# Layer 1 of a hybrid decoder trunk: weight copies ordered ahead of a rounding, and a last output block in two groups with three stores per row tile

## The chip, the cores and the metric

The kernel runs on one core of a Trainium2 chip. A core has five engines, each with an instruction stream of its own that it works off in order: TensorE (PE, matrix products into banks of the accumulator memory), VectorE (DVE), ScalarE (ACT), GpSimd (POOL) and SyncE (SP, which here issues transfers only). Transfers (DMA) are issued to a queue by one of the engines. The metric is the time of one execution on the device in microseconds; the median of several runs is given.

## The reference

Two layers are applied to `x` (256 rows, 1024 columns), and then a last RMS norm. Each layer normalises its input, multiplies it with one 1024 x 3584 matrix, and feeds three kinds of heads: eight attention heads A with a dilated mask, an RG-LRU recurrence B of 256 channels, and four stick-breaking attention heads C. Their gated outputs are joined, multiplied with a 1024 x 1024 matrix and added to the input.

```python
def hybrid_layer(x, cos, sin, norm_gain, w_in, ...):
    hn = rms_norm(x, norm_gain)
    proj = jnp.einsum('bsd,de->bse', hn, w_in)
    a_q, a_k, a_v, a_g, b_x, b_g, c_q, c_k, c_v, c_g = jnp.split(proj, _in_split_points(), axis=-1)
...
    y_a = dilated_attention(qa, ka, va)... * jax.nn.silu(a_g)
    y_b = rg_lru_branch(b_x, ...) * jax.nn.silu(b_g)
    y_c = stick_breaking_attention(qc, kc, vc)... * jax.nn.silu(c_g)
    y = jnp.concatenate([y_a, y_b, y_c], axis=-1)
    return x + jnp.einsum('bse,ed->bsd', y, w_out)

def reference(x, ..., final_gain):
...
    for l in range(DEPTH):
        h = hybrid_layer(h, ...)
    return rms_norm(h, final_gain)

def rms_norm(x, gain):
    xf = x.astype(jnp.float32)
    xf = xf * lax.rsqrt(jnp.mean(xf * xf, axis=-1, keepdims=True) + EPS)
    return (xf * gain.astype(jnp.float32)).astype(x.dtype)
```

## The kernel before

**Tiling.** The 256 rows are two tiles of 128 (`t`), the 1024 columns eight blocks of 128 (`k`). Every operand of a large product is split into a rounded half (`hi`) and the remainder (`lo`), and `mm3` adds three products: hi x hi, hi x lo, lo x hi. In the projections of layer 1 (`l == 0` in the code; layer 2 is `l == 1`) the result of 256 columns for all rows sits in one bank, two blocks of 128 columns beside each other.

**Weights.** They come as 18 chunks a layer, 1 MB each. `load_chunk` takes a chunk in two loads of 512 KB on SP's queue, into a ring of five staging buffers `st` (pool `wst`). ACT rounds each in two pieces of 512 columns (`whi`, line 109), and DVE subtracts to get the rest (`wlo`, line 110). A staging buffer is free for the next load when both of its pieces are subtracted; SP's queue is in order. Chunks are asked for two ahead of their use (`ask`, `AHEAD`).

**Order.** PE's instructions run in the order of the code. Those of the other engines are put in order by a scheduler with a model of the durations; `dep(a, b)` adds an edge, so that `a` is put behind `b`. `table` loads one of ACT's two function tables.

**The place in layer 1.** After the first query and key chunks of A, `split_qk` rounds q and k, `conv` projects the input of the LRU (`bxp`) and convolves it on DVE, and meanwhile PE transposes the stick-breaking weights `sw` (`turned`, lines 458 to 463). Each of three `turned` groups fills a bank `s` (pool `at`, four banks), which ACT copies to `wv` (line 463). Then `second` runs the dilated scores (`dil_scores`, line 514), which take four `s` banks. `it`, `th`, `rt` belong to the LRU, whose gates (line 573) also take `s` banks.

**The end of layer 2.** The output product has 1024 rows of weights, taken in two halves (`out_mm`; first the outputs of B and C with half of A, then the rest), and 512 columns at a time (`n2`). The first halves of all four blocks `(t, n2)` come ahead of the second ones, so four banks stay open: one of pool `at`, three of pool `pp`; pool `yp` has one bank `y`, used by the value products (line 426) and read by line 412. When a block is done, DVE adds it to the residual `xres` (line 689) and `finish` makes the last norm: ACT squares and sums, DVE multiplies with the gain, ACT takes the logarithm and the exponential for the root (`lnv`, `rstd`, line 83), then DVE scales the first 512 columns and ACT the last 512, and SP and ACT store them (line 244). For the very last block the residual is added in two pieces of 320 and 192 columns (`LATE`); DVE squares and sums the first piece (line 231), ACT the second (line 232).

Of the kernel before, what the change touches and what calls it, by code (L numbers as in the profile page):

```python
# [15 lines left out]
P = 128  # L16
S = 256
D = 1024
# [10 lines left out]
AHEAD = 2  # L29
WST = 5  # L30
SCR = 7
LATE = 320
WARM = 7

C_DG = 0
# [13 lines left out]
def trunk_kernel(ctx: ExitStack, tc: tile.TileContext, x, first_x, first, wpack, prm_d, gatew, gains, consts, rope, out):  # L49
# [32 lines left out]
    def tab(*a, **k):  # L82
        i = dep(act.activation(*a, **k), loaded["load"])  # L83
        loaded["users"].append(i)
        return i
# [10 lines left out]

    xx, xh, xl = x_tile()

    split = {}

    def load_chunk(l, c):
        hi = wsp.tile([P, 2048], F32R, name="whi", tag="whi")
        lo = wsp.tile([P, 2048], F32R, name="wlo", tag="wlo")
        for i in range(2):
            st = wst.tile([P, 1024], F32, name="st", tag="st")
            nc.sync.dma_start(out=st, in_=wpack[l, c][:, i * 1024:(i + 1) * 1024])
            for j in range(0, 1024, 512):
                ws, ss = slice(i * 1024 + j, i * 1024 + j + 512), slice(j, j + 512)
                split[l, c] = act.activation(hi[:, ws], st[:, ss], AF.Copy)  # L109
                dve.tensor_sub(lo[:, ws], st[:, ss], hi[:, ws].bitcast(F32))  # L110
        return hi, lo

# [91 lines left out]
        act.activation(hi, ps, AF.Copy)  # L204
        dve.tensor_sub(lo, ps, hi.bitcast(F32))

    def mm3(ps, lhs, rhs, ks, first, last):
        lh, ll = lhs
        rh, rl = rhs
        seq = [(a, b, k) for a, b in ((lh, rh), (lh, rl), (ll, rh)) for k in ks]  # L210
        for i, (a, b, k) in enumerate(seq):
            pe.matmul(ps, a(k), b(k), start=first and i == 0, stop=last and i == len(seq) - 1)  # L212

    last = {}

    def finish(t, n2):
        ot = last["ot", t, n2] = scr(512)
        x_t = xres[:, t, n2 * 512:n2 * 512 + 512]
        if n2 == 0:
            sq = wk.tile([P, 3], F32, name="sq3", tag="sq3", bufs=2)  # L220
            last["sq", t] = sq, wk.tile([P, 1], F32, name="ss", tag="ss", bufs=2)
        sq, ss = last["sq", t]
        if n2 == 0:
            act.activation(scr(512), x_t, AF.Square, accum_out=sq[:, 0:1])
            gps.tensor_scalar(ss, sq[:, 0:1], 1.0 / D, EPS, ALU.mult, ALU.add)
            dve.tensor_mul(ot, x_t, last["gf"][:, 0:512])
            return
        c, late = 0, ss
        if t == 1:
            c, late = LATE, sq[:, 2:3]  # L230
            dve.tensor_tensor_reduce(scr(c), x_t[:, 0:c], x_t[:, 0:c], 1.0 / D, ss, ALU.mult, ALU.add, late)
        act.activation(scr(512 - c), x_t[:, c:512], AF.Square, scale=D ** -0.5, accum_out=sq[:, 1:2])
        dve.tensor_mul(ot, x_t, last["gf"][:, 512:1024])
        ln = wk.tile([P, 1], F32, name="lnv", tag="lnv", bufs=2)
        tab(ln, sq[:, 1:2], AF.Ln, bias=late)
        rstd = wk.tile([P, 1], F32, name="rstd", tag="rstd", bufs=4)
        tab(rstd, ln, AF.Exp, scale=-0.5)
        for half, queue in ((0, nc.sync), (1, act)):
            o = last["ot", t, half]
            if half == 0:  # L240
                dve.tensor_scalar(o, o, rstd, None, ALU.mult)
            else:
                act.activation(o, o, AF.Copy, scale=rstd)  # L243
            queue.dma_start(out=out[t * P:(t + 1) * P, half * 512:half * 512 + 512], in_=o)

    def normed(t):
        rstd = rms_stats(t, gps)
# [50 lines left out]
    for l in range(L):  # L298
# [14 lines left out]
        def proj_b(c, mid=None, to=None, sc=1.0):  # L313
            pair = c in PAIRED[l]
            hi, lo = [a.rearrange("p (k c) -> p k c", c=256) for a in weights(l, c, AHEAD - 1 if mid else AHEAD)]
            if pair:
                flat = None if to is not None else scr(512)
                to = [v2(flat)[:, b, :] for b in range(2)] if to is None else to
            else:
                flat = bank(pp, "pp")  # L320
            for b in range(2):
                cs = slice(b * P, b * P + P)
                if pair:
                    ps = bank(pp, "pp")
                    seq = [(0, k) for k in range(NK - 1)] + [(1, k) for k in range(NK)] + [(0, NK - 1)]
                    for i, (is_lo, k) in enumerate(seq):
                        if is_lo:
                            pe.matmul(ps[:, 0:S], lo[:, k, cs], xh[:, k, :], start=False, stop=False,  # L328
                                      skip_group_check=True)
                        else:  # L330
                            pe.matmul(ps, hi[:, k, cs], xx[:, k].rearrange("p h t -> p (h t)"), start=i == 0,  # L331
                                      stop=i == len(seq) - 1, skip_group_check=True)
                    low = wk.tile([P, S], F32, name="low", tag="low", bufs=2)
                    act.activation(low, ps[:, S:2 * S], AF.Copy, scale=sc)  # L334
                    if sc == 1.0:
                        dve.tensor_add(to[b], ps[:, 0:S], low)
                    else:
                        dve.scalar_tensor_tensor(to[b], ps[:, 0:S], sc, low, ALU.mult, ALU.add)
                else:
                    mm3(flat[:, b * 256:(b + 1) * 256], [lambda k, a=a: a[:, k, cs] for a in (hi, lo)],  # L340
                        [lambda k, a=a: a[:, k, :] for a in (xh, xl)], range(NK), True, True)
                if b == 0 and mid:
                    mid()
                    ask(l, c)
            return flat
# [111 lines left out]
        def turned(tiles, h0, gs, to):  # L457
            for g in gs:
                tp = bank(at, "s")
                for i in range(4):  # L460
                    h, j = divmod(4 * g + i, 3)
                    pe.transpose(tp[:, i * P:(i + 1) * P], tiles[h0 + h][:, j * P:(j + 1) * P], ident)  # L462
                act.activation(to[g], tp, AF.Copy)

        def turned_tile():
            wv = wk.tile([P, 1536], F32, name="wv", tag="wv", bufs=1)
# [148 lines left out]
        split_qk(0, ("yl0", "yh0"))  # L615
        sw_t, sw_heads = turned_tile()
        conv(lambda: turned(sw, 0, (0,), sw_t))
        turned(sw, 0, (1, 2), sw_t)
        y_c = {}

        def second():
# [28 lines left out]
        table(SIGM)  # L650
        silu(ag[:, 0:2, :], ps)
        emit_y(y_c["y"], ag[:, 0:2, :], 4, 2)
        silu(ag[:, 2:4, :], proj_b(CH_AG + 1))
        table(LN_EXP)

        def out_mm(ps, w, t, half, ks, first, last):
            v = [a.rearrange("p (k c) -> p k c", c=512) for a in w]
            ts_ = slice(t * P, t * P + P)
            mm3(ps, [lambda k, a=a: a[:, k, ts_] for a in ys[half]],
                [lambda k, a=a: a[:, k, :] for a in v], ks, first, last)  # L660

        o_ps = {}
        for n2 in range(2):
            w = weights(l, CH_O + n2)
            for t in range(NT):
                o_ps[t, n2] = bank(at, "s") if (t, n2) == (0, 0) else bank(pp, "pp")
                out_mm(o_ps[t, n2], w, t, 0, range(4), True, False)
                if (t, n2) == (0, 0):
                    y_c["p"] = dil_transposes(4)
                if (t, n2) == (0, 1):  # L670
                    emit_y(values(va, y_c["p"], 4), ag[:, 2:4, :], 6, 2)
# [4 lines left out]
        for t in range(NT):  # L676
            if t == 1 and l == 0:
                next_x = x_tile()
                xn0 = normed(0)
            for n2 in range(2):  # L680
                cs = slice(n2 * 512, n2 * 512 + 512)
                for ks in ((0, 1), (2, 3)):
                    out_mm(o_ps[t, n2], ow[n2], t, 1, ks, False, ks[0] == 2)
                    if (l, t, n2, ks[0]) == (0, 1, 1, 0):
                        turn(xn0, 0, *next_x[1:])
                parts = ((0, LATE), (LATE, 512)) if l > 0 and (t, n2) == (1, 1) else ((0, 512),)
                for c0, c1 in parts:
                    c = slice(n2 * 512 + c0, n2 * 512 + c1)
                    dve.tensor_add(xres[:, t, c], o_ps[t, n2][:, c0:c1], xres[:, t, c])  # L689
                if l > 0:  # L690
                    finish(t, n2)

# [106 lines left out]
```

## Time and profile before

| | us |
|---|---|
| median of three runs | 248.68 (248.48 to 250.25) |
| the profiled execution, whole | 248.61 |
| its span, first to last instruction | 246.5 |
| PE busy / DVE busy / ACT busy in the span | 238.6 / 193.3 / 170.5 |
| POOL busy | 11.3 |
| mean granted clock of PE, as a share of full speed | 0.995 |

The profile is one execution. A row of the chain or of the timeline begins with the start and the length in microseconds, both counted from the span's beginning; then come the engine, the operation with its line in the kernel, the output and input by their names in the program, the shapes and the count of equal instructions. A bracket at the end gives how long the engine had idled before and what released it. PEld is PE's weight load, and SPq, ACTq and POOLq are the engines' issuing of transfers. The chain follows the work that ended last back to the start, and so shows what set the time; the groups sum over the whole span and show only what is much.

### The profile page before, as it was taken

The numbers are of one execution on the slowest core, as the hardware profiler recorded it, in microseconds if no ns is written. First come the engines' busy times: TensorE is split into PE (matmuls) and PEld (weight loads), VectorE is DVE, ScalarE is ACT, GpSimd is POOL, SyncE is SP. The second block draws the span as 40 slices with busy tenths as digits, with TensorE's granted clock in tenths as the row PEclk, the third lists the DMA queues.
The fourth block names the chain that finished last, engine by engine and source line by source line (L and its number), as shares of the span: only waits on it lengthen the run. The fifth ranks groups of instructions, "written<-read, shape, count | busy, mean of one in ns | idle before, by whom it ended". The sixth has DMA issues, their size and how long they took to land.

```text
span 246.5 us, 4741 instructions
## 1 busy us (share of the span) xinstructions
PE 238.6 (97%) x1753; PEld 212.4 (86%) x1753; DVE 193.3 (78%) x454; ACT 170.5 (69%) x368; POOL 11.3 (5%) x45
## 2 busy tenths in 40 slices
PE   7999999999999999999999999999999999999990
PEld 4889999999998899878889988888889889987870
DVE  3875599999999789986693666999999967985253
ACT  3867989854688499974672775876589749992142
POOL 0027100000100000000000000000010000000000
PEclk9999999999999999999999999999999999999997
DMA  6999799377737632277258387506462752000022
GB/s 208 390 289 412 313 316 322 112 237 255 229 102 233 231 96 78 89 237 251 108 166 256 101 297 256 201 6 204 148 205 56 233 228 85 3 0 0 3 85 85
DMA packets 13174, 43.90 MB, mean 178 GB/s; under 512 B 1632, under 2 KB 2144, under 8 KB 13152
## 3 DMA queue, kind: packets, MB, share of 16 engines
q1 hardware_dynamic: 12384, 42.30, 50.9%
q10 hardware_dynamic: 576, 0.79, 0.9%
q0 software_dynamic: 192, 0.52, 0.8%
q8 instruction: 14, 0.23, 0.3%
q14 instruction: 8, 0.07, 0.1%
HBM read 42.03 MB, written 1.05 MB: 175 GB/s over the span
## 4 chain that ended last, share of the span: by engine, by line
PE 94%; DMA 2%; DVE 1%; ACT 1%; SPq 0%; issue 0%; ACTq 0%
PE pp L212 51%; PE pp L331 11%; PE s L212 9%; PE pp L328 5%; PE s L169 4%; PE s L462 3%; PE s L514 2%; PE y L426 2%; DMA st<-first 2%; PE pp L169 2%; PE s L442 1%; PE pp L426 1%; PE s L573 1%; PE s L260 1%; DVE xres L689 0%; ACT scr L243 0%
## 5 line engine op out<-in xcount | busy, mean ns | idle before, releaser
L110 DVE TENSOR_TENSOR wlo<-st,whi 128x512 fp32r<-128x512 f32 x132 | 84.0, 684 | 12.6 <-ACT whi L109 12.3
L109 ACT ACTIVATE whi<-st 128x512 fp32r<-128x512 f32 x132 | 73.8, 628 | 20.2 <-DMA st<-w_pack 7.5
L212 PE MATMUL pp<-xx,whi 128*128 128x256 f32 x480 | 63.8, 285 | 0.0
L212 PEld LDWEIGHTS pp<-xx,whi 128*128 128x128 f32 x480 | 59.7, 191 | 1.3 <-ACT whi L109 0.4
L212 PE MATMUL pp<-xx,wlo 128*128 128x256 f32 x240 | 33.7, 283 | 0.0
L212 PEld LDWEIGHTS pp<-xx,wlo 128*128 128x128 f32 x240 | 31.0, 192 | 0.0
L331 PE MATMUL pp<-xx,whi 128*128 128x512 f32 x112 | 29.2, 396 | 0.0
L331 PEld LDWEIGHTS pp<-xx,whi 128*128 128x128 f32 x112 | 20.1, 189 | 3.9 <-ACT scr L83 0.3
L83 ACT ACTIVATE pr<-scr,mn 128x128 f32<-128x128 f32 (+1 forms) x32 | 14.1, 442 | 8.4 <-DVE mn L521 8.4
L77 ACT ACT_TABLE_LOAD x13 | 16.7, 1283 | 1.9 <-PEq L792 1.7
L328 PEld LDWEIGHTS pp<-xx,wlo 128*128 128x128 f32 x112 | 15.3, 190 | 1.1
L328 PE MATMUL pp<-xx,wlo 128*128 128x256 f32 x112 | 15.6, 282 | 0.0
L212 PE MATMUL pp<-whi,yh 128*128 128x512 f32 x48 | 14.4, 400 | 0.0
L212 PE MATMUL pp<-wlo,yh 128*128 128x512 f32 x48 | 13.8, 390 | 0.0
L212 PE MATMUL pp<-whi,yl 128*128 128x512 f32 x48 | 13.8, 389 | 0.0
L212 PEld LDWEIGHTS pp<-wlo,yh 128*128 128x128 f32 x48 | 9.0, 188 | 1.9
L212 PEld LDWEIGHTS pp<-whi,yl 128*128 128x128 f32 x48 | 9.0, 188 | 1.9
L212 PEld LDWEIGHTS pp<-whi,yh 128*128 128x128 f32 x48 | 8.6, 188 | 1.9 <-issue 0.3
L414 ACT ACTIVATE yh<-scr 128x512 fp32r<-128x512 f32 x8 | 5.1, 631 | 7.3 <-DVE scr L412 7.2
L169 PE MATMUL s<-whi,xx 128*128 128x512 f32 (+1 forms) x36 | 9.6, 384 | 0.2
L521 DVE CUSTOM_DVE_ANT_0 scr<-s,con 128x128 f32<-128x128 f32 (+1 forms) x32 | 9.2, 351 | 0.0
L334 ACT ACTIVATE low<-pp 128x256 f32<-128x256 f32 x14 | 5.3, 376 | 5.1 <-PE pp L331 5.1
(175 smaller groups left out, 357.4 us busy)
## 6 DMA issues: line engine op xcount, KB each, us to landing
st<-w_pack SPq DMA_DIRECT2D x66, 512.0 KB, 5.0
st<-first SPq DMA_DIRECT2D x7, 512.0 KB, 5.7
xres<-x_in SPq DMA_DIRECT2D x2, 512.0 KB, 8.7
gw_t<-gate_w SPq DMA_DIRECT2D x2, 256.0 KB, 7.7
gn<-gains SPq DMA_DIRECT2D x1, 512.0 KB, 6.2
xs<-xc POOLq DMA_DIRECT2D x4, 128.0 KB, 4.8
gf<-gains SPq DMA_DIRECT2D x1, 512.0 KB, 6.8
out<-scr SPq DMA_DIRECT2D x2, 256.0 KB, 2.1
```

Of the source, the lines that this page charges most:

```text
L77: load = act.preload_act_table_set(name)
L83: i = dep(act.activation(*a, **k), loaded["load"])
L109: split[l, c] = act.activation(hi[:, ws], st[:, ss], AF.Copy)
L110: dve.tensor_sub(lo[:, ws], st[:, ss], hi[:, ws].bitcast(F32))
L169: pe.matmul(ps[t][:, c0 - base:c1 - base], a[:, k, t * P:(t + 1) * P], b[:, c0:c1], start=k == 0 and i == 0 and c0 == base, stop=k == NK - ...
L212: pe.matmul(ps, a(k), b(k), start=first and i == 0, stop=last and i == len(seq) - 1)
L328: pe.matmul(ps[:, 0:S], lo[:, k, cs], xh[:, k, :], start=False, stop=False, skip_group_check=True)
L331: pe.matmul(ps, hi[:, k, cs], xx[:, k].rearrange("p h t -> p (h t)"), start=i == 0, stop=i == len(seq) - 1, skip_group_check=True)
L334: act.activation(low, ps[:, S:2 * S], AF.Copy, scale=sc)
L426: pe.matmul(y[hr, p * 128 + o:p * 128 + 256], vt[:, s0, hs], wts[i][s0], start=s0 == 0, stop=s0 == 1)
L462: pe.transpose(tp[:, i * P:(i + 1) * P], tiles[h0 + h][:, j * P:(j + 1) * P], ident)
L521: dve.tensor_tensor_reduce(xs[:, cs], sps[h][:, cs], nmask[:, cs], -0.125, 3e38, ALU.add, ALU.min, mn[:, t:t + 1])
```

## The change

Four things are altered.

1. `rounds` keeps all roundings of a chunk, and in layer 1 an edge puts the first rounding of the second key chunk of A behind the last of the three copies of line 463.
2. For the last block `(t, n2) = (1, 1)` of layer 2, the 512 columns become two groups of 256, in both halves of the product. One has the bank `y`. The other has one half of the bank that held the second projection of A's gate (`seeded`); ACT first copies the residual of these 256 columns there, and the products are added on top, so no addition of the residual follows. In the first half of the product the seeded group goes first, in the second it goes last. So that the bank adds onto the copy, the projection of an unpaired chunk gives its start flag for the first of its two blocks only.
3. `finish` is rewritten. Its output tile is one buffer of 1024 columns from the staging pool. ACT does all squares, the last of them from the seeded bank; POOL adds the partial sums; DVE's square-and-sum of 320 columns is gone. The gain multiply of the seeded piece reads the bank too.
4. Each row tile is stored in three pieces: columns 0 to 256 by SP, 640 to 1024 by ACT, 256 to 640 by SP. DVE scales the first and the third of these, ACT the second.

```diff
-LATE = 320
+LATE = 256
+STORE = (0, 256, 640, 1024)
...
                 split[l, c] = act.activation(hi[:, ws], st[:, ss], AF.Copy)
+                rounds.setdefault((l, c), []).append(split[l, c])
...
-    def finish(t, n2):
-        ot = last["ot", t, n2] = scr(512)
-        x_t = xres[:, t, n2 * 512:n2 * 512 + 512]
+    def finish(t, n2, ps=None, c0=0, c1=512):
         if n2 == 0:
+            last["ot", t] = wst.tile([P, 1024], F32, name="st", tag="st")
...
+        cs = slice(n2 * 512 + c0, n2 * 512 + c1)
+        x_t = xres[:, t, cs] if ps is None else ps
+        i = n2 + (c0 > 0)
+        act.activation(scr(c1 - c0), x_t, AF.Square, scale=D ** -0.5, accum_out=sq[:, i:i + 1])
+        dve.tensor_mul(ot[:, cs], x_t, last["gf"][:, cs])
         if n2 == 0:
-            act.activation(scr(512), x_t, AF.Square, accum_out=sq[:, 0:1])
-            gps.tensor_scalar(ss, sq[:, 0:1], 1.0 / D, EPS, ALU.mult, ALU.add)
-            dve.tensor_mul(ot, x_t, last["gf"][:, 0:512])
-            return
-        c, late = 0, ss
-        if t == 1:
-            c, late = LATE, sq[:, 2:3]
-            dve.tensor_tensor_reduce(scr(c), x_t[:, 0:c], x_t[:, 0:c], 1.0 / D, ss, ALU.mult, ALU.add, late)
-        act.activation(scr(512 - c), x_t[:, c:512], AF.Square, scale=D ** -0.5, accum_out=sq[:, 1:2])
-        dve.tensor_mul(ot, x_t, last["gf"][:, 512:1024])
...
-        for half, queue in ((0, nc.sync), (1, act)):
...
+            gps.tensor_scalar(ss, sq[:, 0:1], EPS, None, ALU.add)
+        elif c1 < 512:
+            gps.tensor_add(ss, ss, sq[:, 1:2])
+        else:
+            ln = wk.tile([P, 1], F32, name="lnv", tag="lnv", bufs=2)
+            tab(ln, sq[:, i:i + 1], AF.Ln, bias=ss)
+            rstd = wk.tile([P, 1], F32, name="rstd", tag="rstd", bufs=4)
+            tab(rstd, ln, AF.Exp, scale=-0.5)
+            for j, queue in ((0, nc.sync), (2, act), (1, nc.sync)):
+                c = slice(*STORE[j:j + 2])
+                if j < 2:
+                    dve.tensor_scalar(ot[:, c], ot[:, c], rstd, None, ALU.mult)
+                else:
+                    act.activation(ot[:, c], ot[:, c], AF.Copy, scale=rstd)
+                queue.dma_start(out=out[t * P:(t + 1) * P, c], in_=ot[:, c])
...
-                        [lambda k, a=a: a[:, k, :] for a in (xh, xl)], range(NK), True, True)
+                        [lambda k, a=a: a[:, k, :] for a in (xh, xl)], range(NK), b == 0, True, True)
...
-        turned(sw, 0, (1, 2), sw_t)
+        copied = turned(sw, 0, (1, 2), sw_t)
+        if l == 0:
+            dep(rounds[l, CH_AK[1]][0], copied)
...
-        silu(ag[:, 2:4, :], proj_b(CH_AG + 1))
+        seeded = proj_b(CH_AG + 1)
+        silu(ag[:, 2:4, :], seeded)
...
+        if l > 0:
+            seed = seeded[:, 0:512 - LATE]
+            act.activation(seed, xres[:, 1, 512 + LATE:1024], AF.Copy)
         for n2 in range(2):
             w = weights(l, CH_O + n2)
             for t in range(NT):
+                if l > 0 and (t, n2) == (1, 1):
+                    tail = [(bank(yp, "y")[:, 0:LATE], 0, LATE), (seed, LATE, 512)]
+                    for ps, c0, c1 in tail[::-1]:
+                        out_mm(ps, w, t, 0, range(4), c0 == 0, False, c0, c1, c0 > 0)
+                    continue
...
+                if tail and (t, n2) == (1, 1):
+                    for ps, c0, c1 in tail:
+                        out_mm(ps, ow[n2], t, 1, range(4), False, True, c0, c1, c0 > 0)
+                        if c0 == 0:
+                            x_t = xres[:, t, 512:512 + LATE]
+                            dve.tensor_add(x_t, ps, x_t)
+                        finish(t, n2, None if c0 == 0 else ps, c0, c1)
+                    continue
```

The order of the instructions moves at two places in layer 1 and at the end. The names there carry buffer numbers: `whi_753` and `wlo_754` are the second key chunk of A (two loads, `st_755` and `st_761`), `whi_921` the chunk of C's gate, `whi_966` that of B's gate, `wv_720` the copied stick-breaking weights, and `qk3` the rounded q and k. On ACT, from the second key chunk's roundings on, this stands before:

```order
L109 ACTIVATE whi_753<-st_755 128x512 x2
L109 ACTIVATE whi_753<-st_761 128x512 x2
L77 ACT_TABLE_LOAD
L499 ACTIVATE qk3_714<-q0_525 128x256
L109 ACTIVATE whi_921<-st_923 128x512 x2
L109 ACTIVATE whi_921<-st_929 128x512 x2
L499 ACTIVATE qk3_717<-k0_644 128x512
L463 ACTIVATE wv_720<-s_747 128x512
L109 ACTIVATE whi_966<-st_968 128x512 x2
L109 ACTIVATE whi_966<-st_974 128x512
L463 ACTIVATE wv_720<-s_802 128x512
L463 ACTIVATE wv_720<-s_808 128x512
```

and now:

```order
L110 ACTIVATE whi_753<-st_755 128x512
L110 ACTIVATE whi_753<-st_761 128x512 x2
L78 ACT_TABLE_LOAD
L502 ACTIVATE qk3_714<-q0_525 128x256
L502 ACTIVATE qk3_717<-k0_644 128x512
L465 ACTIVATE wv_720<-s_747 128x512
L465 ACTIVATE wv_720<-s_802 128x512
L465 ACTIVATE wv_720<-s_808 128x512
L110 ACTIVATE whi_753<-st_755 128x512
L110 ACTIVATE whi_921<-st_923 128x512 x2
L110 ACTIVATE whi_921<-st_929 128x512 x2
L110 ACTIVATE whi_966<-st_968 128x512 x2
```

One rounding of the second key chunk and all those of the two gate chunks now stand behind the three copies. On DVE the same stretch reads before:

```order
L110 TENSOR_TENSOR wlo_754<-st_761,whi_753 128x512
L500 TENSOR_TENSOR qk3_717<-k0_644,qk3_717 128x512
L110 TENSOR_TENSOR wlo_754<-st_761,whi_753 128x512
L110 TENSOR_TENSOR wlo_922<-st_923,whi_921 128x512 x2
L110 TENSOR_TENSOR wlo_922<-st_929,whi_921 128x512
L391 SCALAR_TENSOR_TENSOR bxp_328<-pp_722,rb_293 128x2x256
L110 TENSOR_TENSOR wlo_922<-st_929,whi_921 128x512
L560 TENSOR_SCALAR xc_329<-bxp_328,prm_t_264 128x256 x2
L562 SCALAR_TENSOR_TENSOR xc_329<-bxp_328,prm_t_264,xc_329 128x256 x6
```

and now:

```order
L112 TENSOR_TENSOR wlo_754<-st_761,whi_753 128x512 x2
L503 TENSOR_TENSOR qk3_717<-k0_644,qk3_717 128x512
L393 SCALAR_TENSOR_TENSOR bxp_328<-pp_722,rb_293 128x2x256
L563 TENSOR_SCALAR xc_329<-bxp_328,prm_t_264 128x256 x2
L565 SCALAR_TENSOR_TENSOR xc_329<-bxp_328,prm_t_264,xc_329 128x256 x2
L112 TENSOR_TENSOR wlo_754<-st_755,whi_753 128x512
L565 SCALAR_TENSOR_TENSOR xc_329<-bxp_328,prm_t_264,xc_329 128x256 x4
L112 TENSOR_TENSOR wlo_922<-st_923,whi_921 128x512 x2
L112 TENSOR_TENSOR wlo_922<-st_929,whi_921 128x512 x2
```

The LRU's input and convolution now stand ahead of the gate chunk's subtractions. At the kernel's end ACT has, before (rows of the last block):

```order
L224 ACTIVATE scr,sq_3073<-xres 128x512
L232 ACTIVATE scr,sq_3073<-xres 128x192
L83 ACTIVATE lnv<-sq_3073 128x1
L83 ACTIVATE rstd<-lnv 128x1
L243 ACTIVATE scr<-scr,rstd 128x512
L244 DMA out<-scr 128x512
```

and now:

```order
L229 ACTIVATE scr,sq_3087<-xres 128x512
L229 ACTIVATE scr,sq_3087<-xres 128x256
L229 ACTIVATE scr,sq_3087<-pp 128x256
L84 ACTIVATE lnv<-sq_3087,ss 128x1
L84 ACTIVATE rstd<-lnv 128x1
L245 ACTIVATE st<-st,rstd 128x384
L246 DMA out<-st 128x384
```

The squares of 320 columns that DVE made are ACT's, in a piece of 256, and the last piece of squares reads the bank itself.

More of the change, by code (lines that the diff above doesn't have):

```diff
@@ L97, in trunk_kernel @@
     xx, xh, xl = x_tile()
-    split = {}
+    split, rounds = {}, {}
     def load_chunk(l, c):
@@ L205, in split_psum, with mm3 @@
         dve.tensor_sub(lo, ps, hi.bitcast(F32))
-    def mm3(ps, lhs, rhs, ks, first, last):
+    def mm3(ps, lhs, rhs, ks, first, last, skip=False):
         lh, ll = lhs
@@ L211, in mm3 @@
         for i, (a, b, k) in enumerate(seq):
-            pe.matmul(ps, a(k), b(k), start=first and i == 0, stop=last and i == len(seq) - 1)
+            pe.matmul(ps, a(k), b(k), start=first and i == 0, stop=last and i == len(seq) - 1,
+                      skip_group_check=skip)
     last = {}
-    def finish(t, n2):
-        ot = last["ot", t, n2] = scr(512)
-        x_t = xres[:, t, n2 * 512:n2 * 512 + 512]
+    def finish(t, n2, ps=None, c0=0, c1=512):
         if n2 == 0:
+            last["ot", t] = wst.tile([P, 1024], F32, name="st", tag="st")
@@ L220, in finish @@
             sq = wk.tile([P, 3], F32, name="sq3", tag="sq3", bufs=2)
             last["sq", t] = sq, wk.tile([P, 1], F32, name="ss", tag="ss", bufs=2)
+        ot = last["ot", t]
         sq, ss = last["sq", t]
-        if n2 == 0:
-            act.activation(scr(512), x_t, AF.Square, accum_out=sq[:, 0:1])
-            gps.tensor_scalar(ss, sq[:, 0:1], 1.0 / D, EPS, ALU.mult, ALU.add)
-            dve.tensor_mul(ot, x_t, last["gf"][:, 0:512])
-            return
-        c, late = 0, ss
-        if t == 1:
-            c, late = LATE, sq[:, 2:3]
-            dve.tensor_tensor_reduce(scr(c), x_t[:, 0:c], x_t[:, 0:c], 1.0 / D, ss, ALU.mult, ALU.add, late)
@@ L232, in finish @@
-        act.activation(scr(512 - c), x_t[:, c:512], AF.Square, scale=D ** -0.5, accum_out=sq[:, 1:2])
-        dve.tensor_mul(ot, x_t, last["gf"][:, 512:1024])
[L234 to L237, printed above, removed]
-        for half, queue in ((0, nc.sync), (1, act)):
[L239 to L244, printed above, removed]
+        cs = slice(n2 * 512 + c0, n2 * 512 + c1)
@@ L462, in turned @@
                     pe.transpose(tp[:, i * P:(i + 1) * P], tiles[h0 + h][:, j * P:(j + 1) * P], ident)
-                act.activation(to[g], tp, AF.Copy)
+                copy = act.activation(to[g], tp, AF.Copy)
+            return copy
         def turned_tile():
@@ L652, in trunk_kernel, with out_mm @@
         emit_y(y_c["y"], ag[:, 0:2, :], 4, 2)
-        silu(ag[:, 2:4, :], proj_b(CH_AG + 1))
+        seeded = proj_b(CH_AG + 1)
+        silu(ag[:, 2:4, :], seeded)
         table(LN_EXP)
-        def out_mm(ps, w, t, half, ks, first, last):
+        def out_mm(ps, w, t, half, ks, first, last, c0=0, c1=512, skip=False):
             v = [a.rearrange("p (k c) -> p k c", c=512) for a in w]
@@ L659, in out_mm @@
             mm3(ps, [lambda k, a=a: a[:, k, ts_] for a in ys[half]],
-                [lambda k, a=a: a[:, k, :] for a in v], ks, first, last)
+                [lambda k, a=a: a[:, k, c0:c1] for a in v], ks, first, last, skip)
         o_ps = {}
+        tail = []
+        if l > 0:
+            seed = seeded[:, 0:512 - LATE]
+            act.activation(seed, xres[:, 1, 512 + LATE:1024], AF.Copy)
         for n2 in range(2):
@@ L685, in trunk_kernel @@
                         turn(xn0, 0, *next_x[1:])
[L686 to L689, printed above, removed]
+                dve.tensor_add(xres[:, t, cs], o_ps[t, n2], xres[:, t, cs])
                 if l > 0:
```

## The prediction

> **What bounds the kernel now.** I read the page's engine line first, then the chain that ended last, then the waits of PE's weight loads, then the timeline around the one wait found and around the end.
>
> ```profile
> PE 238.6 (97%) x1753; PEld 212.4 (86%) x1753; DVE 193.3 (78%) x454; ACT 170.5 (69%) x368; POOL 11.3 (5%) x45
> ```
>
> PE is busy for 238.6 of 246.5 us, so a gain has to come out of PE's own stretch or out of what follows its last matmul. The chain in order of time shows both (start, length, what):
>
> ```profile
> 58.19 1.93 PE s L514 x37
> 60.13 14.58 PE pp L212 x120
> ...
> 112.56 2.72 PE s L212 x12
> ...
> 175.60 1.37 PE s L514 x38
> ...
> 240.11 0.02 issue
> 240.13 0.77 DVE xres L689 x2
> ...
> 240.92 0.46 ACT scr L232 x2
> ...
> 241.45 0.30 ACT lnv L83
> ...
> 241.78 0.20 ACT rstd L83
> ...
> 242.05 0.72 ACT scr L243
> ```
>
> Two things stand out. The attention scores of line 514 are the same work each time, yet the first group took 1.93 us and the one at 175.60 took 1.37: 0.56 us too much. And from PE's end at 240.11 to the span's end at 246.5 there are 6.4 us in which nothing overlaps. The rest of PE is back to back: 120 matmuls of 256 columns in 14.58 us are 121.5 ns each, 12 of 512 columns in 2.72 us are 227 ns each.
>
> The long first group has its reason in the waits (weight loads of PE, us in total, times, longest):
>
> ```profile
> PEld s L514 <- ACT wv L463: 0.2, 1, 0.2
> ```
>
> The weight load shows only 0.2 us of idle engine, as the load sits half done, but the names tell it: the scores need the banks that line 463 copies out. The timeline there:
>
> ```profile
> 54.28 1.04 PE L462 MATMUL s<-con,sw 128*128 128x128 f32 x8
> 54.35 2.49 DVE L110 TENSOR_TENSOR wlo<-st,whi 128x512 fp32r<-128x512 f32 x4
> ...
> 57.05 0.63 ACT L109 ACTIVATE whi<-st 128x512 fp32r<-128x512 f32 x1 [1.05 <-DMA st<-w_pack]
> ...
> 57.59 1.06 ACT L463 ACTIVATE wv<-s 128x512 f32<-128x512 f32 x2
> ```
>
> PE ends its transposes at 55.32, but the copies run at 57.59 to 58.65: ACT takes its work in order, and ahead of them stood a rounding that sat 1.05 us for a weight load. PE wanted the banks at 58.19.
>
> **Part 1, the order on ACT in the first layer.** The dependency names one rounding, but the order shows the scheduler pulling the last two copies ahead of eight. The copies then wait for the transposes alone: 55.32 plus 1.06 us is 56.4, well before 58.19. I take the whole 0.56 us as gained (ends: 0 and 0.56).
>
> What is late next: one first rounding of the second key chunk (`whi_753`), its subtraction on DVE, and the buffer that this frees for a load.
>
> ```profile
> 52.81 0.33 SPq L106 DMA_DIRECT2D st<-w_pack  x1
> ...
> 63.03 2.08 PE L212 MATMUL pp<-xx,whi 128*128 128x256 f32 x16
> ...
> 63.39 0.28 DVE L521 CUSTOM_DVE_ANT_0 scr<-s,con 128x128 f32<-128x128 f32 x1
> ...
> 76.09 1.06 ACT L463 ACTIVATE pa<-s 128x512 f32<-128x512 f32 x2
> ...
> 78.81 0.43 PE L573 MATMUL s<-xc,gw_t 64*64 64x256 f32 x2
> ```
>
> The rounding now ends about 57.0 (56.4 plus 0.6), its subtraction about 57.3; PE uses the chunk first at 63.03 less 0.56, so 5 us of cover. The load that waits for this buffer goes from SP at 57.3 and not 52.81; SP's queue is in order, so the loads behind it move by up to 4.5 us, but they are for chunks that PE reaches from 74 us on. DVE loses nothing: the row of four subtractions at 54.35 stood ahead of `bxp`, whose projection PE had ended before the transposes of 54.28; now `bxp` and the convolution run in that place, and the subtractions after them. Adding up the new DVE order from the rows' starts puts line 521 at about 63.0, against 63.39. On POOL the move of `xs` follows the convolution and comes earlier. Cost of all this: nothing, bounded by rival D.
>
> **Part 2, the last 512 columns as two groups.** The twelve matmuls of 512 columns in each of the two halves become 24 of 256: 24 x 121.5 ns = 2.92 us for 2.72, so +0.20 each, +0.40 in all, both on PE's path, as PE waits for nothing there. The Trainium skill, TensorE: Matmul & The Clock Gate, section Back-to-back issue gap, gives N/2.4 + 2.5 ns for a warm array, so 109 ns for 256 columns and 216 for 512. By it the cost would be 24 x 109 less 12 x 216, about +0.03 each, and the forecast 0.3 us lower; the trace has 121.5 and 227, and the trace decides.
>
> The seed is one more ACT copy of 256 columns into a bank. Nearest rows and its cover:
>
> ```profile
> L334 ACT ACTIVATE low<-pp x14: 361/383/385, 145.9 to 187.8; 128x256 f32<-128x256 f32 x14
> ...
> 226.32 0.69 DVE L412 TENSOR_TENSOR scr<-y,ag 128x512 f32<-128x512 f32 x1 [2.35 <-PE y L426]
> ...
> 227.04 0.63 ACT L414 ACTIVATE yh<-scr 128x512 fp32r<-128x512 f32 x1 [4.04 <-DVE scr L412]
> ```
>
> About 0.38 us, in front of work that ends 4.04 us before ACT is next needed: nothing on the path; without that cover it would cost its 0.4. The `y` bank is free only when DVE has read it, at 227.01, 0.69 us after PE released that reading; but the seeded group goes first on PE and takes 12 x 121.5 ns = 1.46 us: hidden; without it some 0.7.
>
> **Part 3, the end.** Rows of the tail, and of the windows (length, five engines' busy time, granted clock, DMA share, GB/s):
>
> ```profile
> 238.14 0.63 ACT L224 ACTIVATE scr<-xres 128x512 f32<-128x512 f32 x1 [0.55 <-DVE xres L689]
> ...
> 240.92 0.36 ACT L232 ACTIVATE scr<-xres 128x192 f32<-128x192 f32 x1 [2.06 <-DVE xres L689]
> ...
> 242.01 0.49 DVE L241 TENSOR_SCALAR scr<-scr,rstd 128x512 f32<-128x512 f32 x1
> 242.05 0.72 ACT L243 ACTIVATE scr<-scr,rstd 128x512 f32<-128x512 f32 x1
> 242.53 0.34 SPq L244 DMA_DIRECT2D out<-scr  x1
> 242.81 0.35 ACTq L244 DMA_DIRECT2D out<-scr  x1
> ```
> ```profile
> out<-scr SPq DMA_DIRECT2D x2, 256.0 KB, 2.1
> out<-scr ACTq DMA_DIRECT2D x2, 256.0 KB, 2.4
> ```
> ```profile
> 239.80:243.30 3.50, 0.29 (x2) 0.00 (x0) 2.31 (x6) 1.68 (x5) 0.00 (x0) 1.00 0.00 0
> 243.30:245.00 1.70, 0.00 (x0) 0.00 (x0) 0.00 (x0) 0.00 (x0) 0.00 (x0) 0.65 0.81 308
> ```
>
> - Both residual additions leave the path: Square starts about 0.02 us after PE instead of at 240.92, so -0.79.
> - Square has 256 columns, not 192, and reads the bank. From 0.36 (192) and 0.63 (512), 0.84 ns a column: +0.05. From a bank it may be 0.03 less or, unseen, a little more.
> - ACT's last scaling has 384 columns, not 512: 128 x 0.84 ns = -0.11. The other operations (Ln, Exp) stay. The gain multiply of the seeded bank is made to wait for Square; it runs beside Ln and Exp (0.5 us with gaps, against 0.4) and ACT scales 0.8 us after Square. The first group's addition, Square and POOL addition have 1.46 us of PE's last group to run in.
> - So the ACT store goes 0.85 us sooner after PE's end. DVE scales 256 columns, then 384, and SP's second store is issued about 0.1 us after ACT's, as SP needs 0.34 us for its first. In the trace both stores' data moved in 0.81 x 1.70 = 1.38 us, from 0.8 us after the first issue. The same bytes in three pieces I take at the same 1.4 us, and the first piece leaves DVE after 256 columns, some 0.1 us ahead: net 0. Ends: -0.2 (an earlier start counts) and +0.7 (a third piece costs as much as each of the two did, 1.38 / 2).
>
> The t = 0 half issues three stores in place of two near 237, six us ahead of the end: covered.
>
> **The sum.** -0.56 + 0.40 - 0.79 + 0.05 - 0.11 + 0 = -1.01 us. The profiled execution took 248.61 us (span 246.5 and 2.1 around it), 0.07 under the median of 248.68 of the runs. 248.61 - 1.01 = 247.6 us, 0.4% less.
>
> **Rivals.** *B: the 0.56 us do not reach the end.* PE comes earlier and then waits for a producer that does not. The tightest place:
>
> ```profile
> 86.16 2.20 ACT L109 ACTIVATE whi<-st 128x512 fp32r<-128x512 f32 x4 [2.66 <-PE pp L212]
> ...
> 97.22 0.63 ACT L414 ACTIVATE yh<-scr 128x512 fp32r<-128x512 f32 x1 [0.17 <-DVE scr L412]
> ...
> 98.44 1.09 PE L212 MATMUL s<-whi,yh 128*128 128x512 f32 x4
> ```
>
> `yh` ends at 97.85, 0.59 us ahead of its matmul. For B: that is as much as the shift. Against it: ACT was itself released by PE at 86.16 after 2.66 us of idling, so it comes earlier too. B gives 247.6 + 0.56 = 248.2 us.
>
> *C: three stores cost more than two*, by +0.7 as bounded above: 248.3 us. For it: ACT's store, issued 0.28 us after SP's, landed 0.3 us slower, so they share what carries them. Against: the bytes are the same. The Trainium skill, DMA: Bandwidth & Descriptors, section Rules for kernel authors, says that spreading transfers over issuing engines brings no bandwidth and that small ones should be joined; by that rule C would be the case, and the rows above agree with the first half.
>
> *D, slower than before:* ACT's copies at 76.09 stand behind a rounding whose load is issued at 70.77 and is issued about 0.8 us later now (one more subtraction ahead on DVE).
>
> ```profile
> 70.77 0.33 SPq L106 DMA_DIRECT2D st<-w_pack  x1
> 74.53 1.66 ACT L109 ACTIVATE whi<-st 128x512 fp32r<-128x512 f32 x3
> ...
> st<-w_pack SPq DMA_DIRECT2D x66, 512.0 KB, 5.0
> ```
>
> PE's line 573 needs a bank back at 78.81 - 0.56 = 78.25; rounding and two copies need 0.6 + 1.06, so the load must land by 76.6, 5.0 us after 71.6. In the trace its data was there by 75.6 at the latest, 4.9 us after its issue, in an otherwise empty queue. Each us over 5.0 is a us of PE; from 6.1 us on all is given back. At 6.4: 249.0 us. The median load of 5.0 speaks for it, the empty queue against.
>
> **Chances.** Forecast 0.68, B 0.16, C 0.11, D 0.05. The range goes from 246.8 (the forecast with the early store, the page's matmul times and the run-to-run spread of some 0.2) to 248.7, which takes in B and C and a run like those of before; D is left out. A measurement of this kernel tells about 1% from no change, 2.5 us. None of the cases reaches it: faster 0.03, same 0.94, slower 0.03.
>
> **What would show each step.** Right: the first group of line 514's scores takes about 1.37 us in the chain, no wait for `wv`; all later PE pieces come 0.56 us sooner; the two 24-matmul groups take 2.9 us; Square begins at once after the last matmul; ACT's last store is issued about 1.9 us after PE's end, where it was 2.70. Wrong: a new PE wait at 78 or 98 us (D, B), a last landing over 2.4 us after its issue (C), or 24 small matmuls at another pace than 121.5 ns.

## The result, and the profile after

The changed kernel takes 247.06 us (median of 22 runs, 246.38 to 247.79); the kernel before took 248.60 us in its own 22 runs (247.00 to 250.25). The ratio is 0.9934, with a 95% interval of 0.9918 to 0.9951, so between 1.2 and 2.0 us less. The forecast was 247.6 us (range 246.8 to 248.7). The medians differ by 1.54 us, half a microsecond more than the forecast's 1.01.

The profiled execution of the changed kernel took 247.45 us as a whole and 245.6 us of span, against 248.61 and 246.5: 1.16 us less. Its engines are as busy as before:

```profile
PE 237.7 (97%) x1777; PEld 213.1 (87%) x1777; DVE 193.3 (79%) x454; ACT 170.8 (70%) x371; POOL 12.4 (5%) x46
```

TensorE's busy time is 0.9 us lower, but that is not the gain: 0.64 us of it lie ahead of the row-scale products near 31.7 us, where TensorE idled more in this execution, and 0.58 us are the stall, which counts as busy; the end added 0.30 us. The chain that ended last shows what was gained. From the kernel before, three more of its rows (start, length, what):

```profile
31.71 0.44 PE y L378 x4
...
226.27 2.94 PE pp L212 x12
229.22 2.72 PE s L212 x12
```

and the changed kernel's chain, where line numbers are 2 to 3 higher:

```profile
31.64 0.44 PE y L380 x4
...
58.12 1.37 PE s L517 x39
59.48 14.59 PE pp L214 x120
...
225.64 1.62 PE pp L214 x12
227.26 1.44 PE y L214 x12
228.70 2.75 PE s L214 x12
...
236.89 1.43 PE y L214 x12
238.32 1.45 PE pp L214 x12
239.77 0.02 issue
239.79 0.48 ACT scr L229 x2
```

The rows cut the execution at the same places of the program, so the difference can be taken piece by piece. "Row-scale products" are the four small products into bank `y` near 31.7 us (line 378, now 380), the last landmark ahead of the place of part 1.

| from, to | before | after | difference |
|---|---|---|---|
| span's start, row-scale products | 31.71 | 31.64 | -0.07 |
| row-scale products, first group of scores | 26.48 | 26.48 | 0.00 |
| the group itself | 1.94 | 1.36 | -0.58 |
| its end, first half of the last block | 166.14 | 166.16 | +0.02 |
| that half | 2.95 | 3.06 | +0.11 |
| the second halves, to TensorE's end | 10.89 | 11.07 | +0.18 |
| TensorE's end, end of the execution (248.61 - 240.11; 247.45 - 239.77) | 8.50 | 7.68 | -0.82 |
| sum | 248.61 | 247.45 | -1.16 |

Part 1, seen in the timeline of ScalarE and VectorE in the changed kernel:

```profile
54.84 1.09 ACT L465 ACTIVATE wv<-s 128x512 f32<-128x512 f32 x2 [1.61 <-PE s L464]
55.81 4.28 ACT L110 ACTIVATE whi<-st 128x512 fp32r<-128x512 f32 x8
...
62.98 0.28 DVE L524 CUSTOM_DVE_ANT_0 scr<-s,con 128x128 f32<-128x128 f32 x1
```

The copies now wait for TensorE's transposes and for nothing else, and end at 55.93, more than 2 us ahead of the scores. The eight roundings follow without a gap or a wait for a load, and the first operation of line 524 stands at 62.98, where adding up VectorE's new order had given 63.0.

The end, in the same kernel's timeline and its answer on transfers (KB each, us from issue to landing):

```profile
241.31 0.81 SPq L246 DMA_DIRECT2D out<-st  x2
241.57 0.35 ACTq L246 DMA_DIRECT2D out<-st  x1
```
```profile
out<-st ACTq DMA_DIRECT2D x1, 192.0 KB, 2.0
out<-st SPq DMA_DIRECT2D x1, 192.0 KB, 2.4
out<-st SPq DMA_DIRECT2D x1, 128.0 KB, 1.9
```

ScalarE's store is issued 1.80 us after TensorE's end, where it was 2.70. The three pieces land 1.9 to 2.4 us after their issue, the last of them SP's second. That one is issued near 241.31 + 0.81 - 0.35 = 241.77 and so lands 4.4 us after TensorE's end. Before, the last landing was that of ScalarE's store, 2.70 + 2.4 = 5.1 us after it.

### The profile page after: what moved, and what is told of

It is laid out like the page before. It is cut to its first block, busy times and chain, and to the rows that moved or that the text cites. A ratio compares the mean times of both kernels' runs of the same rounds, so it can differ in the third digit from the quotient of the medians.

```text
span 245.6 us, 4797 instructions
## 1 busy us (share of the span) xinstructions
PE 237.7 (97%) x1777; PEld 213.1 (87%) x1777; DVE 193.3 (79%) x454; ACT 170.8 (70%) x371; POOL 12.4 (5%) x46
## 4 chain that ended last, share of the span: by engine, by line
PE 94%; DMA 2%; DVE 1%; ACT 0%; SPq 0%; issue 0%; DVEq 0%; ACTq 0%
PE pp L214 50%; PE pp L333 11%; PE s L214 9%; PE pp L330 5%; PE s L171 4%; PE s L464 3%; PE y L428 2%; DMA st<-first 2%; PE s L517 2%; PE pp L171 2%; PE s L444 1%; PE y L214 1%; PE pp L428 1%; PE s L576 1%; PE s L262 1%; DVE wlo L164 0%
## 5 line engine op out<-in xcount | busy, mean ns | idle before, releaser
L214 PE MATMUL pp<-whi,yh 128*128 128x512 f32 (+1 forms) x48 | 13.3, 382 | 0.0
L214 PE MATMUL pp<-wlo,yh 128*128 128x512 f32 (+1 forms) x48 | 12.8, 372 | 0.0
L214 PE MATMUL pp<-whi,yl 128*128 128x512 f32 (+1 forms) x48 | 12.8, 372 | 0.0
```

## The experiments

Two things were open: why the runs gained 1.5 us where the trace shows 1.2, and which of the parts carries how much. Four kernels first: the kernel before again, each of the two halves of the change alone, and the change with two stores.

**The kernel before, again** (no edit).

> The kernel before, unchanged, against itself. Both theories: the same time, ratio 1.000 within about 0.003. What it is to tell is the stall at line 514 in another execution. Theory 'the stall varies': the first group of scores takes another time than the 1.93 us of the first profile, anywhere from 1.4 to 2.9 us, because it hangs on the landing of a weight load. Theory 'the stall is fixed': 1.9 us again, within 0.1.

**The edge alone**, on the kernel before.

```diff
+                rounds.setdefault((l, c), []).append(split[l, c])
...
-        turned(sw, 0, (1, 2), sw_t)
+        copied = turned(sw, 0, (1, 2), sw_t)
+        if l == 0:
+            dep(rounds[l, CH_AK[1]][0], copied)
```

> The kernel before with the edge in layer 1 alone. Forecast: the first group of line 514 takes 1.37 us, all later pieces of TensorE come 0.56 us sooner, the tail is as before: -0.56 us, about 248.0, ratio 0.9977. Theory 'the stall varies and was larger in the median run': -1.0 us, ratio 0.996, with a narrower spread than the kernel before. Theory 'the surplus lies in the end': -0.56 us.

**The end alone**: the changed kernel without that edge.

```diff
-        if l == 0:
-            dep(rounds[l, CH_AK[1]][0], copied)
```

> The changed kernel without the edge in layer 1. By the two traces so far: the two groups of 24 cost +0.30 us, the last landing comes 0.80 us sooner after TensorE's end: -0.5 us, about 248.1, ratio 0.998, and the stall at line 514 is there again with the spread of the kernel before. Theory 'the surplus lies in the end': -1.0 us, ratio 0.996.

**Two stores** in the changed kernel.

```diff
-STORE = (0, 256, 640, 1024)
+STORE = (0, 512, 1024)
...
-            for j, queue in ((0, nc.sync), (2, act), (1, nc.sync)):
+            for j, queue in ((0, nc.sync), (1, act)):
...
-                if j < 2:
+                if j < 1:
```

> The changed kernel with two stores of 512 columns in place of three. Forecast term (net 0 for the third store, but 512 columns on ScalarE's last scaling): last landing 0.1 us later after TensorE's end than in the changed kernel, +0.1 us, ratio to before 0.994. Rival 'three stores cost': it is faster than the changed kernel by up to 0.7 us, ratio 0.991. Rival 'the early piece pays': last landing 0.3 us later, +0.3 us, ratio 0.995.

Measured against the kernel before: itself 0.9994 (0.9974 to 1.0014); the edge alone 0.9947 (0.9927 to 0.9967), 1.3 us less; the end alone 0.9970 (0.9946 to 0.9993), 0.75 us less; with two stores 0.9943 (0.9922 to 0.9964), which these times don't tell from three. So the end fits its forecast of about 0.5 us, and the edge alone gained more than 0.56 us, even at the near end of its interval (0.8 us). Its nine runs also lie closer together than those of the kernel before (247.0 to 247.8 us), but other kernels with the new order spread wider (with two stores 246.6 to 249.0), so the spread tells nothing. Why the edge gained so much, the second profile of the kernel before says. Its chain:

```profile
31.08 0.44 PE y L378 x4
...
57.56 0.42 PE s L514 x4
...
58.02 0.48 PE s L514 x2
...
58.51 1.42 PE s L514 x31
59.92 14.58 PE pp L212 x120
```

The scores begin 0.63 us sooner than in the first profile, as the row-scale products do, yet the next stage begins at 59.92 against 60.13. TensorE came early and was held up twice within the group; the group took 2.36 us. In the timeline of ScalarE in that profile, the rounding that stands ahead of the copies:

```profile
56.85 0.63 ACT L109 ACTIVATE whi<-st 128x512 fp32r<-128x512 f32 x1 [1.61 <-DMA st<-w_pack]
57.39 1.06 ACT L463 ACTIVATE wv<-s 128x512 f32<-128x512 f32 x2
```

It started 0.20 us sooner than the 57.05 of the first profile, while TensorE was 0.63 us sooner. In both profiles the group of scores ends 1.47 to 1.48 us after the second copy does (60.13 after 58.65, 59.92 after 58.45). By this reading the stall is what is left between a load's landing and TensorE's arrival, and no fixed cost.

**A pad ahead of the stall** tests that. The two row-scale products are made three times over, in both kernels, with the same result.

```diff
-                pe.matmul(rb_ps[:, t * P:(t + 1) * P], ones, dg, start=True, stop=True)
+                for _ in range(3):
+                    pe.matmul(rb_ps[:, t * P:(t + 1) * P], ones, dg, start=True, stop=True)
```

> The kernel before with 0.88 us more of TensorE work ahead of the stall: the two products that spread the row scales (0.44 us at 31.71) are made three times. Theory 'line 514 waits for a load that lands by its own clock': its group ends near 59.9 us as in the three traces with the old order (60.12, 59.93, 59.81), unless TensorE alone takes it past that; the stall shrinks to 0 to 0.1 us and the time grows by the pad less the stall, 0 to 0.6 us. Theory 'the stall is a fixed cost of the order': the stall stays at 0.3 to 1.0 us and the time grows by 0.88 us.

> The changed kernel with the same 0.88 us of TensorE work. Theory 'load with its own clock': no stall is left to take it up, so from the row-scale products to the end of line 514's group it takes 27.85 us plus 0.88, that is 28.73, and the time grows by 0.88 us over the changed kernel's. Theory 'fixed cost': also 0.88. The two theories differ in the kernel before; here the number is the price of the pad.

The chains, of the padded kernel before and of the padded changed kernel:

```profile
32.04 1.34 PE y L379 x12
...
59.41 1.37 PE s L515 x39
60.78 14.59 PE pp L212 x120
```
```profile
30.73 1.34 PE y L381 x12
...
58.11 1.37 PE s L518 x39
59.48 14.59 PE pp L214 x120
```

From the row-scale products to the end of the scores it is 28.74 and 28.75 us, 27.85 and the pad's 0.90. No stall is left in the kernel before either, as its TensorE now comes after the copies; the "fixed cost" of 0.3 to 1.0 us is not there. How much stall the pad took up this trace cannot tell, though: its row-scale products begin late, at 32.04, and the fourth profile below, which begins at 32.06 without a pad, has a stall of only 0.16 us. The times lean the same way: the padded kernel before is at 1.0013 of the kernel before (0.9986 to 1.0039), some 0.3 us for the pad, and the padded changed kernel at 0.9984 (0.9960 to 1.0008) where the change had 0.9934, some 1.2 us. The difference of the two prices, 0.9 us, is about as large as its uncertainty.

**Two more profiles of the kernel before**, to see how large the stall is as a rule.

> The kernel before, a third profile. Theory 'load with its own clock': the end of line 514's first group less 27.85 us and less the start of the row-scale products is the stall; the group ends at 59.8 to 60.2 us whatever the start, so the stall is about 32.1 less that start: 1.0 us at 31.1, 0.4 at 31.7, none from 32.1 on. Rival 'fixed cost': 0.56 us whatever the start.

> The kernel before, a fourth profile, as the third. If the stall of these two and of the second profile is mostly near 1 us, the first profile (0.56) was a low sample, and the median gain of the edge is larger than the forecast's 0.56 us; if it is near 0.5 us, the surplus of the measured gain stays open.

Their chains, of the third and the fourth:

```profile
30.74 0.45 PE y L378 x4
...
58.41 1.42 PE s L514 x31
59.82 14.58 PE pp L212 x120
```
```profile
32.06 0.45 PE y L378 x4
...
58.54 1.53 PE s L514 x34
60.07 14.59 PE pp L212 x120
```

and of the kernel with the end alone, whose order in layer 1 is the old one, and of the one with the edge alone:

```profile
31.65 0.45 PE y L380 x4
...
59.80 14.59 PE pp L214 x120
```
```profile
30.60 0.44 PE y L379 x4
...
58.45 14.59 PE pp L213 x120
```

| profile | row-scale products | end of the scores | between | stall (over 27.85) |
|---|---|---|---|---|
| before, first | 31.71 | 60.13 | 28.42 | 0.57 |
| before, second | 31.08 | 59.92 | 28.84 | 0.99 |
| before, third | 30.74 | 59.82 | 29.08 | 1.23 |
| before, fourth | 32.06 | 60.07 | 28.01 | 0.16 |
| the end alone | 31.65 | 59.80 | 28.15 | 0.30 |
| the change | 31.64 | 59.48 | 27.84 | 0 |
| the edge alone | 30.60 | 58.45 | 27.85 | 0 |

With the old order the landmark varies by 1.3 us and the end of the scores by 0.3; with the new one both move together. In the five profiles with the old order the late rounding starts at 57.05, 56.85, 56.75, 57.00 and 56.73 us, and the scores end 1.46 to 1.48 us after the second copy. So the rival "fixed cost" falls, and the end of the scores goes by the landing; what keeps that landing so steady was not followed further back. The four profiles of the kernel before have a mean stall of 0.74 us, and the first was below it. The mean of four is a rough one, and the edge alone gained somewhat more than that in its runs: the stalls explain about 0.2 of the 0.4 us that the runs gained beyond the trace's 1.16, and the rest is inside the interval (1.2 to 2.0 us) but not shown.

**Is it that one load?** Here the edge is put on the two roundings of the load that ScalarE sat for, and all else in layer 1 stays in the old order; the end is the new one.

```diff
-                rounds.setdefault((l, c), []).append(split[l, c])
+                if (l, c, i) == (0, CH_BG, 1):
+                    dep(split[l, c], last["copied", l])
...
-        if l == 0:
-            dep(rounds[l, CH_AK[1]][0], copied)
+        last["copied", l] = copied
```

> The changed kernel with the edge put on other roundings: only the two of the second load of B's gate chunk stand behind the copies (the load whose landing ScalarE sat for at 57.05), all else on ScalarE and VectorE in the order of before. Theory 'that one load makes the stall': the copies run at about 56.0 to 57.1, line 514's group takes 1.37 us, and from the row-scale products to its end it is 27.85 us as in the changed kernel; ratio to before 0.9935. Rival 'the wider reorder is needed' (the convolution ahead of the subtractions, the other six roundings): a stall of 0.3 us or more is left.

In its timeline of ScalarE the copies follow the first load's roundings without a gap, and in its chain the stall is gone (27.85 us from the first row to the last):

```profile
54.80 1.14 ACT L110 ACTIVATE whi<-st 128x512 fp32r<-128x512 f32 x2
55.85 1.07 ACT L464 ACTIVATE wv<-s 128x512 f32<-128x512 f32 x2
```
```profile
31.20 0.45 PE y L379 x4
...
57.69 1.37 PE s L516 x39
59.05 14.59 PE pp L215 x120
```

The ratio is 0.9954 (0.9933 to 0.9974), not to be told from the change's. Of the two roundings one stood behind the copies already, so moving one removes the stall as moving eight does; the wider reorder neither helps nor costs anything that shows.

**The end, taken apart.** First without the seed: the second group has a bank of its own, and its residual is added by VectorE.

```diff
-            seed = seeded[:, 0:512 - LATE]
-            act.activation(seed, xres[:, 1, 512 + LATE:1024], AF.Copy)
...
-                    tail = [(bank(yp, "y")[:, 0:LATE], 0, LATE), (seed, LATE, 512)]
+                    tail = [(bank(yp, "y")[:, 0:LATE], 0, LATE), (bank(pp, "pp")[:, 0:512 - LATE], LATE, 512)]
...
-                        if c0 == 0:
-                            x_t = xres[:, t, 512:512 + LATE]
-                            dve.tensor_add(x_t, ps, x_t)
-                        finish(t, n2, None if c0 == 0 else ps, c0, c1)
+                        x_t = xres[:, t, 512 + c0:512 + c1]
+                        dve.tensor_add(x_t, ps, x_t)
+                        finish(t, n2, None, c0, c1)
```

> The changed kernel without the seed: the second group of 256 columns has a bank of its own, and VectorE adds the residual after TensorE's end. Forecast's step: one addition of 256 columns and its gap come back, 0.42 + 0.02 us, so the last scaling's store is issued about 2.25 us after TensorE's end where the changed kernel has 1.80; +0.44 us, ratio to before 0.995. Rival 'the addition was hidden by other work': no change, 1.80.

The chain of that kernel, and ScalarE's store in its timeline:

```profile
239.28 0.02 issue
239.31 0.43 DVE xres L698
```
```profile
241.57 0.35 ACTq L246 DMA_DIRECT2D out<-st  x1
```

The store comes 2.29 us after TensorE's end, against 1.80 with the seed and 2.25 expected. The addition is back on the path at its full length of 0.43 us, and the kernel's ratio is 0.9962 (0.9938 to 0.9985).

The end of the two-store kernel, whose TensorE ends at 241.24 (timeline of ScalarE, and its transfers):

```profile
243.15 0.35 ACTq L246 DMA_DIRECT2D out<-st  x1
```
```profile
out<-st ACTq DMA_DIRECT2D x1, 256.0 KB, 2.4
```

Its last store is issued 1.91 us after TensorE's end and lands 2.4 us later, 4.3 us in all. With three, the last to land is SP's second, 4.4 us after TensorE's end, the same within these roundings. The third store neither costs 0.7 us, as rival C had it, nor shortens the path by much; the ratio of 0.9943 says the same, where rival C asked for 0.991. Measured from TensorE's end to the end of the whole execution it is 7.77 us with two stores (249.01 - 241.24) and 7.68 with three.

**The added GpSimd addition**, made by VectorE instead.

```diff
-            gps.tensor_add(ss, ss, sq[:, 1:2])
+            dve.tensor_add(ss, ss, sq[:, 1:2])
```

> The changed kernel with the one added GpSimd addition of the partial sums made by VectorE. From the last landing to the end of the span it was 1.26, 1.27 and 1.23 us in the traces with the old end and 1.50, 1.48 and 1.64 in those with the new one. Theory 'the added GpSimd instruction costs at the very end': 1.26 us again, -0.25 us, ratio 0.9925 or less. Rival 'the new stores or buffers cost it': 1.5 us still, no change to the changed kernel.

TensorE ends at 238.95 here (the chain has the "issue" row there), the span at 244.3: 5.35 us, against 5.83 in the changed kernel (245.6 - 239.77). That looks like half a microsecond. But the whole execution took 246.46 us, 2.16 us more than its span, while the changed kernel's took 1.85 us more than its span. To the end of the execution it is 7.51 us against 7.68, and the ratio is 0.9936 (0.9915 to 0.9957), no better than the change. Two thirds of what the span lost came back outside it, and that is no accident of one execution: in its twelve runs the time outside the span is 2.08 to 2.17 us, in the 22 of the changed kernel 1.79 to 1.89. So the theory falls for the most part; a gain of 0.2 us would still lie inside the interval.

**An early load**, in the hope of a better version. The gates' weights of 256 KB, first read near 78 us, are loaded behind the next two chunks in layer 1.

```diff
-        nc.sync.dma_start(out=gw_t, in_=gatew[:, l, :])
+        if l > 0:
+            nc.sync.dma_start(out=gw_t, in_=gatew[:, l, :])
...
             cq_ps = proj_b(CH_CQ)
+            nc.sync.dma_start(out=gw_t, in_=gatew[:, l, :])
```

> The changed kernel with the gate weights of the LRU (256 KB, first read at 78 us) loaded behind the next two weight chunks in layer 1 instead of ahead of them. Three of ten traces have a wait of up to 0.5 us on the second chunk's rounding near 28.7 us, whose load lands at 25.5 to 27.0; with 256 KB less ahead of it in the queue it lands about 0.6 us sooner. Theory: no such wait, the row-scale products come 22.9 us after the first product of line 171 (or earlier limits of the start), 0 to 0.5 us gained where the wait was, and all of it reaches the end now that line 517 no longer waits: ratio to before 0.9915 to 0.9935. Rival: the wait was rare enough that nothing shows, 0.9935.

0.9946 (0.9923 to 0.9969): nothing shows. Its chain has no wait near 28.7 us, but the profile of the change had none there either. No kernel was found that measurably beats the change.

## Why the prediction held, point by point

The range reached up to 248.7 us and so took in the time of the kernel before as well; that the measured time lies in it says little. What bears the prediction out are the steps that it named, one by one. It also took 1%, 2.5 us, for the least that can be told from no change; the runs show 0.7%, with an interval of 0.5% to 0.8%.

**Part 1.** Place, cause and cure were as forecast: the copies stood behind a rounding that sat for a load, they now end at 55.93 (forecast 56.4), the group takes 1.37 us, and all that follows comes sooner (-0.63 us at 225.64, with the 0.07 of the start). SP's next issue, for the buffer that comes free later, is at 57.29 (forecast 57.3). Moving eight roundings cost nothing that shows against moving one. The reading of the weight loads was off: the load was said to sit half done, but none of that line's loads between 55 and 90 us lasts longer than 188 ns in that trace. It is the end of the second copy, 1.47 us ahead of the group's end, that ties the stall to the copies. What was wrong is the size of this term, as a statement on the median: the sum took 0.56 us from one profile as the value of the stall. In four profiles of the kernel before it is 0.16 to 1.23 us, 0.74 on the mean, because the load lands by its own clock and the start of TensorE varies. "All later pieces come 0.56 us sooner" is right for a pair of executions with the start of the first profile only.

**Part 2.** Forecast +0.40, measured +0.29 (0.11 and 0.18). The 24 matmuls of the second halves take 1.43 + 1.45 = 2.88 us, 120 ns each, about the 121.5 ns of the row used, and cost 0.18 us for the forecast's 0.20. The first halves cost 0.11: their first twelve take 1.62 us where twelve others take 1.44, and the old first twelve had such a surplus too (2.94 against 2.72), larger by 0.04 us, so this delay at the start of the group is not the change's. The Trainium skill's figure (TensorE: Matmul & The Clock Gate, section Back-to-back issue gap), which the page gives for an isolated matmul and not for a stream of weight loads and matmuls, gave +0.06 for both; the trace lies nearer its own row. The seed's copy and the wait for bank `y` were covered, as forecast: the second group of twelve follows the first without a gap at 227.26.

**Part 3.** Forecast -0.85 us, measured -0.82 to the end of the execution. The closeness is in part luck: ScalarE's store goes 0.90 us sooner, but the last landing only 0.7 us (4.4 after TensorE's end for 5.1), as SP's second store now lands last, and the remaining 0.1 us lies behind the last landing, where the forecast had put nothing. The residual additions were on the path at their length (0.49 us came back for one of 256 columns), Square begins 0.02 us after TensorE's end, and ScalarE's store is issued 1.80 us after it (forecast 1.9). The stores were forecast at 0 between -0.2 and +0.7; the traces have two stores 0.09 us behind three at the end of the execution, so about 0.

**The rivals.** B did not occur: of the 0.58 us of the group 0.56 are still there at 225.64 (0.63 less the start's 0.07). C fell with the two-store kernel. D had its late load: the changed kernel's rounding waits for it, in the timeline of ScalarE,

```profile
75.37 0.63 ACT L110 ACTIVATE whi<-st 128x512 fp32r<-128x512 f32 x1 [0.19 <-DMA st<-w_pack]
75.91 1.06 ACT L465 ACTIVATE pa<-s 128x512 f32<-128x512 f32 x2
```

but it was there by 75.37, not after 76.6, so the copies end 1.3 us ahead of the gates' products at 78.25. Its issue was as late as feared, 71.86 (forecast 71.6), but it was there 3.5 us later and not after the median's 5.0. The Trainium skill's rule on joining transfers (DMA: Bandwidth & Descriptors, section Rules for kernel authors) speaks of many small ones and puts the mark at 64 KB; the pieces here have 128 and 192 KB, so it hardly speaks for rival C, and the trace shows the third store costing nothing.

The forecast came out in its range, half a microsecond high, of which the traces assign 0.1 to part 2 and about 0.2 to the low stall of the one profile that it rested on. The rest stays open.

## What to carry to other kernels

A stall behind a load absorbs what the stages ahead of it gain: with the old order the third profile was 1.3 us ahead of the fourth at the row-scale products and 0.25 us ahead at the end of line 514's scores. Read such a stall as "landing less arrival", and take its size from several executions, not from one; and where an in-order engine serves both loads and a bank that TensorE waits for, putting the bank's copy ahead of the one rounding whose load is late is enough. At a kernel's end, where nothing overlaps, seeding the accumulator with the residual was worth the full length of the addition, against 0.3 us for cutting the block into two groups, which had to be paid for it here.

## What the hardware showed unexpectedly

The first products of line 171 run at one of two paces. Two chains, of the two-store kernel and of the one with the edge alone, with the same two instructions:

```profile
6.06 0.43 PE pp L171 x2
```
```profile
5.56 0.23 PE pp L170 x2
```

215 ns a matmul of 256 columns in the one, 117 in the other, in the one up to 10.3 us, although the profile's granted clock reads 1.00 in both for 4 to 8 us. The Trainium skill (TensorE: Matmul & The Clock Gate, section What's actually happening) has the array at half clock until a window of activity that runs freely has passed, and so a varying number of slow matmuls; from its 1.2 GHz one estimates 213 ns for 256 columns, which agrees with 215. That the gate is the cause no run here shows. These two kernels begin the products of line 171 within 0.4 us of each other (4.87 and 4.51) and reach the row-scale products at 33.10 and 30.60 us, the latest and the earliest of all these profiles: 2.5 us, more than the change is worth.

And the end of the span is not the end of the execution: in all runs with the new end the time outside the span was 1.79 to 1.92 us, with the old end 2.07 to 2.27, and with the new end but without the added GpSimd addition 2.08 to 2.17. So it goes by that one addition and not by the stores; why, the profiles don't show. Two kernels' spans can differ by a few tenths of a microsecond that their times don't.
